# A two-layer hybrid diffusion step: a mark behind the normalisation, modulations shared by halves, and a residual added by DMA

## The chip, the cores and the metric

One core of a Trainium2 chip runs the program. The metric is the device time of one execution in microseconds (us), lower is better; the median of several timed executions is compared.

## The reference

Two layers act on 128 context tokens and 128 latent tokens that share all weights; the model width is 2048 and the feed-forward width 8192, in float32. Cut to what the change touches:

```
mods = silu(cond) @ w_mod[l] + b_mod[l]          # six vectors of 2048 for each kind of token
shift1, scale1, gate1, shift2, scale2, gate2 = mods
h = rms_norm(x, norm1_g) * (1 + scale1) + shift1
mix = concat(gla(h @ w_in), attention(h @ w_in), deltanet(h @ w_in)) @ w_out
x = x + gate1 * mix
h = rms_norm(x, norm2_g) * (1 + scale2) + shift2
x = x + gate2 * (square(relu(h @ w_ff1)) @ w_ff2)
```

`cond` is one vector for the context tokens and one for the latent tokens, so that a modulation is a product of a 2048 x 2048 block of `w_mod` with two vectors. Modulations are numbered m = 0 to 5 in the order above (0 shift1, 1 scale1, 2 gate1, 3 shift2, 4 scale2, 5 gate2); (l, m) is modulation m of layer l. The outputs are x of both kinds of token and the caches and states of the context.

## The kernel before

**Layout and units.** x stays in SBUF, transposed: 16 chunks of 128 model rows by 256 columns, of which the first 128 are context tokens and the last 128 latent ones. A matrix product is made in units of 128 output rows, a unit of the feed-forward in two halves of the contraction. For each half a 512 KB tile `raw` (128x1024) is loaded on SP's queue (`load_half`, six buffers). ACT rounds it to `hi`, DVE forms `lo` = `raw` − `hi` (`split_half`, three buffers each), and PE runs 16 matmuls with `hi` (on the rounded activations and on their remainders) and 8 with `lo`, into the PSUM tile `g` (`gemm_d`). The evacuation of w_out and ff2 (`res_evac`) is DVE's: x += g * gate, one instruction for each kind of token. That of ff1 (`ff_evac`) is three ACT instructions and a DVE subtraction.

**Stages of a layer.** Input projection and the three mixers, then w_out (16 units), a lead stage, and the feed-forward: ff1 in four blocks of 16 units, ff2 in four, in the order ff1(0), ff1(1), ff2(0), ff1(2), ff2(1), ff1(3), ff2(2), ff2(3). In the lead stage (`norm_lead`) PE runs the first six units of ff1 on x as it is before the normalisation (PSUM tile `gl`), and DVE and ACT make the normalised input beside that: `get_rstd` with a Newton iteration of small DVE instructions (`nv`, `n2t`, `n2y`), then `normed`, 16 chunks in each of which DVE makes `ht`, ACT `hu` and the rounded `act`, and DVE the remainder, `act` = `hu` − `act`. The rest of ff1(0) needs those chunks.

**Modulations.** They are filler work, made well before they are needed, on one of two engines. `mod_pe` runs 16 groups on PE, each with two 512 KB loads `raw` from `w_mod` on SP's queue and four matmuls 32x512 (eight rows in the trace); it ends with a small addition of the bias `bm` on DVE. `mod_dv` runs on DVE: for each of two halves of the contraction and each of 16 output chunks it loads a 512 KB tile `mraw` on SP's queue (three buffers) and runs two multiply-and-reduce instructions against the broadcast vectors `sb` (1 MB, one buffer, loaded on POOL's queue at the start of each half). They show as `CUSTOM_DVE_ANT_0 junk` in the trace and as `ISA junk` in the order, 64 for a modulation; the first half starts from `bm` and leaves sums in `part`, the second starts from `part` and writes `modc`. The list `ONDV` says which modulations go to DVE: (0,5), (1,1), (1,0), (1,5).

**What sets the order.** `start_mod` puts a modulation's generator into a queue, `modq` for PE and `modv` for DVE. After every half-unit `tick()` takes one step of each, at the rates in `rate`: for PE R3 = 0.15 in the feed-forward, for DVE V3 = 0.6 in ff1(0) and ff1(1) and V5 = 0.55 behind them; in layer 1 the rate for DVE is 0. All seven modulations of layer 0's feed-forward start behind the first two normalised units of ff1(0): (0,5), then those of layer 1 in the order `FF0M`. `mod_flush` finishes one that is needed. The code's order is only a priority: a scheduler that runs at build time puts each engine's instructions into their final order and may move an instruction whose inputs are there ahead of others. Each engine and queue then runs its own list in order.

Of the kernel before, what the change touches and what calls it, by code (L numbers as in the profile page):

```python
# [17 lines left out]
P = 128  # L18
# [9 lines left out]
V3, V5 = 0.6, 0.55  # L28
FF0M = (1, 0, 5, 2, 4, 3)
MX1M = (4, 3)  # L30
LATE = 3
ONDV = ((0, 5), (1, 1), (1, 0), (1, 5))
# [9 lines left out]
def tile_hybrid_step(ctx: ExitStack, tc: tile.TileContext, A: dict, O: dict):  # L42
# [357 lines left out]
    def mod_dv(l, m, modc, bm):  # L400
        mac = X["mac"]
        part = mdp.tile([P, 16, 2], F32, tag="part", name="part")
        i = ONDV.index((l, m))
        order = [(half, n) for half in range(2) for n in range(16)]
# [7 lines left out]
        for u, (half, n) in enumerate(order):  # L412
# [6 lines left out]
            for c in range(2):  # L419
                junk = mac.tile([P, 1024], BF16, tag="junk", name="junk")  # L420
                ve.tensor_tensor_reduce(
                    out=junk, in0=raw, in1=sb[:, c], scale=1.0,
                    scalar=part[:, n, c : c + 1] if half else bm[:, m, n : n + 1], op0=ALU.mult, op1=ALU.add,
                    accum_out=modc[:, m, n, c : c + 1] if half else part[:, n, c : c + 1],
                )
            yield

    def mod_pe(l, m, modc, bm):
        ps = pmod.tile([P, 512], F32, tag="mod", name="mod")
        tk = newtok()  # L430
        for k in range(16):
            raws = [load_half(A["w_mod"][l, m, k, half]) for half in range(2)]
            for gg in (2, 3, 0, 1):
# [4 lines left out]
                    start=(k == 0),  # L438
# [8 lines left out]
        for r in range(4):  # L447
# [4 lines left out]
            bc(bm[:, m].rearrange("p (g r) -> p r g", r=4), 2),  # L452
# [41 lines left out]
    def normed(rstd, dst, scl, shf):  # L494
        for k in range(16):
# [7 lines left out]
            ve.tensor_tensor(dst[:, k, 256:512], u, dst[:, k, 0:256].bitcast(F32), ALU.subtract)  # L503
# [12 lines left out]
    def start_mod(l, m):  # L516
        modc, s12, bm, ng = mods[l]

        def chain():
            yield from (mod_dv if (l, m) in ONDV else mod_pe)(l, m, modc, bm)  # L520
# [9 lines left out]
        (modv if (l, m) in ONDV else modq).append(g)  # L530
# [112 lines left out]
    for l in range(L):  # L643
# [790 lines left out]
        rate[:] = [R3, 0 if last else V3]  # L1434
# [4 lines left out]
        def ff1(q):  # L1439
            hid = hids[q % 2]  # L1440
            us = [(tsrc(w1, q * 16 + j), ff_evac(hid, j)) for j in range(LEAD if q == 0 else 0, 16)]
            if q == 0:
                d = DL
                gemm_seq(us[:d], lambda k: nact[:, k, 0:512])
                us = us[d:]
                if (l, 5) not in gens:
                    start_mod(l, 5)
                if not last:
                    for m in FF0M:
                        start_mod(l + 1, m)  # L1450
            gemm_seq(us, lambda k: nact[:, k, 0:512])
            return hid

        def ff2(q, hid):
            st = q == 3 and not last
            sc1 = mods[l + 1][1][:, 0] if st else None
            gemm_seq([(tsrc(w2[q], n), res_evac(n, 5, act if st else None, sc1)) for n in range(16)], lambda k: hid[:, k, 0:512], l in WIDE)
# [195 lines left out]
```

## Time and profile before

| | us |
|---|---|
| median of 3 timed runs | 2579.03 |
| lowest and highest | 2578.31, 2583.78 |
| the profiled run | 2589.99 |
| its span (first to last instruction) | 2588.2 |
| its PE, DVE, ACT busy | 2503.7, 1822.5, 1225.7 |

The mean granted TensorE clock of the profiled run is 0.986 of full speed. PE is TensorE's matmuls, PEld its weight loads (they overlap PE), DVE VectorE, ACT ScalarE, POOL GpSimd, SP SyncE. Nearly all instructions are recorded at a few helper lines (L56 for DVE and ACT, L86 for matmuls), so the names of output and inputs tell them apart. Layer 0's w_out stage runs from 506.37 to 606.17 us, its lead to 688.36, its feed-forward to 1410.44; layer 1's w_out stage runs from 1778.71 to 1858.03 and its lead to 1908.97.

### The profile page before, as it was taken

What the parts mean: (1) busy time and instruction counts of PE and PEld (TensorE: products, weight loads), DVE (VectorE), ACT (ScalarE), POOL (GpSimd) and SP (SyncE); (2) the same over time, 40 slices, a digit from 0 to 9 for tenths busy, and PEclk for the clock granted to TensorE, in tenths of its full rate; (3) what the DMA queues carried; (4) which work ended last, traced back from release to release, by engine and by line L of the source; (5) the groups of instructions that cost most, each with busy time, mean ns of one, the idle gap of its engine ahead of it and who ended that gap; (6) DMA issues with size and microseconds to landing.
All of it is one profiled execution on the core that took longest, in us unless ns stands there. A gap on an engine that the chain in (4) does not pass through costs nothing.

```text
span 2588.2 us, 47588 instructions
## 1 busy us (share of the span) xinstructions
PE 2503.7 (97%) x18860; PEld 2250.6 (87%) x18860; DVE 1822.5 (70%) x3510; ACT 1225.7 (47%) x1977; POOL 31.2 (1%) x59
## 2 busy tenths in 40 slices
PE   6999999988799999999999999999999999999999
PEld 4777677778799999999999888898999989999888
DVE  3456767698998889988456767697764565564665
ACT  3356244434655345344344763455575435445433
POOL 1000000000000000000000000000000000000000
PEclk9999999998899999999999999999999999999999
DMA  9875767797799999998777765445556666666664
GB/s 362 313 253 180 274 213 279 274 371 247 241 327 340 326 336 326 333 333 294 235 235 237 245 232 172 141 134 166 176 182 185 185 190 188 185 192 187 185 199 141
DMA packets 171935, 622.00 MB, mean 240 GB/s; under 512 B 20496, under 2 KB 21072, under 8 KB 170688
## 3 DMA queue, kind: packets, MB, share of 16 engines
q1 hardware_dynamic: 165600, 600.12, 68.4%
q0 software_dynamic: 3712, 15.59, 1.7%
q8 instruction: 148, 2.42, 0.4%
q10 hardware_dynamic: 2400, 3.24, 0.4%
q14 instruction: 75, 0.61, 0.1%
HBM read 612.57 MB, written 6.31 MB: 239 GB/s over the span
## 4 chain that ended last, share of the span: by engine, by line
PE 89%; DMA 4%; DVE 3%; ACT 2%; issue 1%; SPq 0%; ACTq 0%; DVEq 0%
PE g L86 67%; PE gt L86 6%; PE mod L86 4%; PE gl L86 4%; DMA raw<-w_mod 2%; DMA raw<-w_tok 1%; DVE lo L56 1%; ACT hi L56 1%; PE ga L86 1%; DVE junk L56 1%; PE eb L86 1%; DMA raw<-w_in 1%; PE fb L86 0%; PE fbm L86 0%; PE ob L86 0%
## 5 line engine op out<-in xcount | busy, mean ns | idle before, releaser
L56 ACT ACTIVATE hi<-raw 128x1024 fp32r<-128x1024 f32 (+1 forms) x742 | 784.5, 1058 | 1104.2 <-PE g L86 791.3
L56 DVE TENSOR_TENSOR lo<-raw,hi 128x1024 fp32r<-128x1024 f32 (+1 forms) x742 | 905.1, 1220 | 431.9 <-ACT hi L56 416.4
L86 PE MATMUL g<-act,hi 128*128 128x256 f32 (+1 forms) x7488 | 1054.1, 291 | 23.9 <-ACT ffr L56 7.4
L86 PEld LDWEIGHTS g<-act,hi 128*128 128x128 f32 x7488 | 955.6, 189 | 100.5 <-ACT hi L56 27.4
L86 PE MATMUL g<-act,lo 128*128 128x256 f32 x4000 | 562.8, 282 | 3.2 <-DVE lo L56 3.2
L86 PEld LDWEIGHTS g<-act,lo 128*128 128x128 f32 x4000 | 516.8, 190 | 14.5 <-DVE lo L56 4.9
L56 DVE SCALAR_TENSOR_TENSOR x<-g,modc,x 128x128 f32<-128x128 f32 x448 | 142.3, 348 | 185.8 <-PE g L86 180.5
L86 PE MATMUL g<-hid,hi 128*128 128x256 f32 (+1 forms) x1536 | 261.3, 319 | 0.0
L86 PEld LDWEIGHTS g<-hid,hi 128*128 128x128 f32 x1536 | 217.1, 188 | 23.1 <-ACT hi L56 5.0
L86 PE MATMUL mod<-raw,sc 128*32 128x512 f32 (+1 forms) x1280 | 152.1, 537 | 28.9 <-DMA raw<-w_mod 25.3
L56 DVE CUSTOM_DVE_ANT_0 junk<-mraw,sb,bm 128x1024 bf16<-128x1024 f32 x128 | 164.0, 1282 | 5.3 <-DMA sb<-scd 2.5
L56 DVE CUSTOM_DVE_ANT_0 junk<-mraw,sb,part 128x1024 bf16<-128x1024 f32 x128 | 164.1, 1282 | 2.1 <-DMA sb<-scd 1.7
L86 PE MATMUL gt<-hi,act 128*128 128x512 f32 x512 | 144.5, 414 | 3.7 <-ACT hi L56 3.7
L86 PE MATMUL g<-hid,lo 128*128 128x256 f32 x1024 | 141.8, 281 | 0.0
L86 PEld LDWEIGHTS g<-hid,lo 128*128 128x128 f32 x1024 | 134.6, 188 | 5.4
L86 PEld LDWEIGHTS gt<-hi,act 128*128 128x128 f32 x512 | 94.6, 192 | 41.1 <-issue 13.7
L86 PEld LDWEIGHTS mod<-raw,sc 128*32 128x32 f32 x1280 | 30.1, 110 | 67.0 <-DMA raw<-w_mod 21.6
L86 PE MATMUL gl<-hid,hi 128*128 128x258 f32 x384 | 74.8, 297 | 4.0 <-ACT hi L56 3.1
L86 PE MATMUL gt<-lo,act 128*128 128x512 f32 x256 | 75.7, 405 | 0.0
L86 PEld LDWEIGHTS gl<-hid,hi 128*128 128x128 f32 x384 | 62.9, 200 | 5.1 <-ACT hi L56 3.7
L86 PE MATMUL gl<-hid,lo 128*128 128x258 f32 x192 | 56.6, 296 | 3.6 <-DVE lo L56 3.6
L86 PEld LDWEIGHTS gt<-lo,act 128*128 128x128 f32 x256 | 48.3, 192 | 10.8 <-issue 0.4
(352 smaller groups left out, 1882.7 us busy)
## 6 DMA issues: line engine op xcount, KB each, us to landing
raw<-w_ff SPq DMA_DIRECT2D x512, 512.0 KB, 4.4
raw<-w_mod SPq DMA_DIRECT2D x256, 512.0 KB, 5.9
mraw<-w_modT SPq DMA_DIRECT2D x128, 512.0 KB, 6.0
raw<-w_in SPq DMA_DIRECT2D x86, 512.0 KB, 4.4
raw<-w_tok SPq DMA_DIRECT2D x64, 512.0 KB, 4.5
raw<-w_out SPq DMA_DIRECT2D x64, 512.0 KB, 4.4
sb<-scd POOLq DMA_DIRECT2D x8, 1024.0 KB, 8.7
raw<-w_in SPq DMA_DIRECT2D x16, 448.0 KB, 6.2
```

The lines of the kernel that those rows point to most:

```text
L56: return f(out, *a, **kw)
L86: i = nc.tensor.matmul(out, lhsT=lhsT, rhs=rhs, start=start, stop=stop, **kw)
```

## The change

Three things change, and two rates with them.

1. A mark. The last subtraction of `normed` and the first multiply-and-reduce instruction of every `mod_dv` get the issue-order token "normed": the scheduler keeps instructions with one token in the order of the code, so a modulation on DVE can't be put ahead of that subtraction.
2. Halves. `mod_dv`, `mod_pe` and `start_mod` take the halves of the contraction they are to make. Of (1,2) DVE makes the first half in layer 0's feed-forward, and PE the second (groups 8 to 15, with `part` added in place of `bm`). Of (1,5), which DVE made whole in layer 0's feed-forward, the second half moves to layer 1's ff1(0), at the new rate V4 = 0.4. V3 becomes 0.65.
3. Adds. In layer 0, ff2 blocks 0 to 2 evacuate with `add_evac`: two ACT copies scaled by the gate write `xd` (128x256, two buffers), and a DMA on POOL's queue adds `xd` to x. The two DVE instructions on x of each of these 48 units are gone.

```diff
--- before.py
+++ after.py
@@ -25,11 +25,11 @@
 TB = 4
 NRAW = 6
 GATES = (4, 5, 6, 7, 0, 1, 2, 3)
-V3, V5 = 0.6, 0.55
-FF0M = (1, 0, 5, 2, 4, 3)
+V3, V5, V4 = 0.65, 0.55, 0.4
+FF0M = ((1, (0, 1)), (0, (0, 1)), (2, (0,)), (5, (0,)), (4, (0, 1)), (3, (0, 1)), (2, (1,)))
 MX1M = (4, 3)
 LATE = 3
-ONDV = ((0, 5), (1, 1), (1, 0), (1, 5))
+ONDV = ((0, 5), (1, 1), (1, 0), (1, 5), (1, 2))
 DL = 2
 WIDE = (1,)
 K0, K1 = 0.4, 0.7
@@ -397,11 +397,15 @@
             if tick():
                 yield
 
-    def mod_dv(l, m, modc, bm):
+    parts = {}
+
+    def mod_dv(l, m, modc, bm, halves):
         mac = X["mac"]
-        part = mdp.tile([P, 16, 2], F32, tag="part", name="part")
+        if 0 in halves:
+            parts[l, m] = mdp.tile([P, 16, 2], F32, tag="part", name="part")
+        part = parts[l, m]
         i = ONDV.index((l, m))
-        order = [(half, n) for half in range(2) for n in range(16)]
+        order = [(half, n) for half in halves for n in range(16)]
 
         def fetch(u):
             raw = mac.tile([P, 1024], F32, tag="mraw", name="mraw", bufs=3)
@@ -418,24 +422,27 @@
             nxt = fetch(u + 1) if u + 1 < len(order) else None
             for c in range(2):
                 junk = mac.tile([P, 1024], BF16, tag="junk", name="junk")
-                ve.tensor_tensor_reduce(
+                i_ = ve.tensor_tensor_reduce(
                     out=junk, in0=raw, in1=sb[:, c], scale=1.0,
                     scalar=part[:, n, c : c + 1] if half else bm[:, m, n : n + 1], op0=ALU.mult, op1=ALU.add,
                     accum_out=modc[:, m, n, c : c + 1] if half else part[:, n, c : c + 1],
                 )
+                if u == 0 and c == 0:
+                    tc.stamp_issue_order_token(i_.ins, "normed")
             yield
 
-    def mod_pe(l, m, modc, bm):
+    def mod_pe(l, m, modc, bm, halves):
         ps = pmod.tile([P, 512], F32, tag="mod", name="mod")
         tk = newtok()
-        for k in range(16):
+        k0 = 8 * halves[0]
+        for k in range(k0, 16):
             raws = [load_half(A["w_mod"][l, m, k, half]) for half in range(2)]
             for gg in (2, 3, 0, 1):
                 mm(
                     ps[32 * gg : 32 * gg + 32, :],
                     sc[:, 2 * k : 2 * k + 32],
                     raws[gg // 2][:, (gg % 2) * 512 : (gg % 2) * 512 + 512],
-                    start=(k == 0),
+                    start=(k == k0),
                     stop=(k == 15),
                     tile_position=(0, 32 * gg),
                     tok=tk,
@@ -449,7 +456,7 @@
         ve.tensor_tensor(
             modc[:, m].rearrange("p (g r) c -> p r g c", r=4),
             pt[:, 0:32].rearrange("p (r g c) -> p r g c", r=4, c=2),
-            bc(bm[:, m].rearrange("p (g r) -> p r g", r=4), 2),
+            parts[l, m].rearrange("p (g r) c -> p r g c", r=4) if k0 else bc(bm[:, m].rearrange("p (g r) -> p r g", r=4), 2),
             ALU.add,
         )
         yield
@@ -500,7 +507,9 @@
                 ve.scalar_tensor_tensor(t[:, s], X["x"][:, k, s], scl[:, k, g : g + 1], rstd[:, s], ALU.mult, ALU.mult)
                 se.activation(u[:, s], t[:, s], AF.Identity, bias=shf[:, k, g : g + 1])
             se.activation(dst[:, k, 0:256], u, AF.Copy)
-            ve.tensor_tensor(dst[:, k, 256:512], u, dst[:, k, 0:256].bitcast(F32), ALU.subtract)
+            i = ve.tensor_tensor(dst[:, k, 256:512], u, dst[:, k, 0:256].bitcast(F32), ALU.subtract)
+            if k == 15:
+                tc.stamp_issue_order_token(i.ins, "normed")
             yield
 
     def norm_lead(srcs, xsp, dst, scl, shf, ldp, sink=None):
@@ -513,11 +522,12 @@
         se.activation(act[:, k, 0:256], src, AF.Copy)
         ve.tensor_tensor(act[:, k, 256:512], src, act[:, k, 0:256].bitcast(F32), ALU.subtract)
 
-    def start_mod(l, m):
+    def start_mod(l, m, halves=(0, 1)):
         modc, s12, bm, ng = mods[l]
+        dv = (l, m) in ONDV and (m != 2 or 0 in halves)
 
         def chain():
-            yield from (mod_dv if (l, m) in ONDV else mod_pe)(l, m, modc, bm)
+            yield from (mod_dv if dv else mod_pe)(l, m, modc, bm, halves)
             if m in (1, 4):
                 j = 0 if m == 1 else 1
                 ve.scalar_tensor_tensor(
@@ -527,7 +537,7 @@
 
         g = chain()
         gens[l, m] = g
-        (modv if (l, m) in ONDV else modq).append(g)
+        (modv if dv else modq).append(g)
         return g
 
     def tsrc(w, n):
@@ -1431,7 +1441,7 @@
 
         norm_lead([tsrc(w1, j) for j in range(LEAD)], hidb, nact, s12[:, 1], modc[:, 3], X["np"],
                   lambda j, t: ff_evac(act, j)(t))
-        rate[:] = [R3, 0 if last else V3]
+        rate[:] = [R3, V4 if last else V3]
         if not last:
             mod_tiles(l + 1)
             layer_consts(l + 1)
@@ -1443,18 +1453,27 @@
                 d = DL
                 gemm_seq(us[:d], lambda k: nact[:, k, 0:512])
                 us = us[d:]
-                if (l, 5) not in gens:
-                    start_mod(l, 5)
+                start_mod(l, 5, (1,) if last else (0, 1))
                 if not last:
-                    for m in FF0M:
-                        start_mod(l + 1, m)
+                    for m, halves in FF0M:
+                        start_mod(l + 1, m, halves)
             gemm_seq(us, lambda k: nact[:, k, 0:512])
             return hid
+
+        def add_evac(n):
+            def f(ps):
+                t = X["np"].tile([P, 256], F32, tag="xd", name="xd", bufs=2)
+                for g in range(2):
+                    s = slice(g * P, g * P + P)
+                    se.activation(t[:, s], ps[:, s], AF.Copy, scale=modc[:, 5, n, g : g + 1])
+                nc.gpsimd.dma_start(x[:, n, :], t, accum_op=ALU.add)
+
+            return f
 
         def ff2(q, hid):
             st = q == 3 and not last
             sc1 = mods[l + 1][1][:, 0] if st else None
-            gemm_seq([(tsrc(w2[q], n), res_evac(n, 5, act if st else None, sc1)) for n in range(16)], lambda k: hid[:, k, 0:512], l in WIDE)
+            gemm_seq([(tsrc(w2[q], n), add_evac(n) if q < 3 and not last else res_evac(n, 5, act if st else None, sc1)) for n in range(16)], lambda k: hid[:, k, 0:512], l in WIDE)
 
         h0 = ff1(0)
         h1 = ff1(1)
```

The order shows where instructions now stand. DVE in layer 0's lead, at the Newton iteration (ISA junk and the small ISA behind it are the modulation); before:

```order
L56 TENSOR_SCALAR nv<-st 128x2
L56 TENSOR_TENSOR lo<-raw,hi 128x1024
L56 ISA junk,modc<-mraw,sb,part 128x1024
L56 ISA modc 128x1
L56 TENSOR_SCALAR n2t<-nv 128x2
L56 ISA junk,modc<-mraw,sb,part 128x1024
L56 ISA modc 128x1
L56 TENSOR_SCALAR n2y<-n2t 128x2
```

and after:

```order
L56 TENSOR_SCALAR nv<-st 128x2
L56 TENSOR_SCALAR n2t<-nv 128x2
L56 TENSOR_SCALAR n2y<-n2t 128x2
L56 SCALAR_TENSOR_TENSOR n2t<-nv,n2y 128x2
L56 TENSOR_TENSOR n2t<-n2t,n2y 128x2
L56 SCALAR_TENSOR_TENSOR n2y<-n2t,n2y 128x2
L56 SCALAR_TENSOR_TENSOR n2t<-nv,n2y 128x2
L56 TENSOR_TENSOR lo<-raw,hi 128x1024
```

The modulation instructions that stood between the Newton steps have moved behind the last subtraction of `normed`; from there to the end of the lead DVE's rows are those of layer 1's lead.

SP's queue around the first load from `w_mod` in layer 0's feed-forward; before:

```order
L408 DMA mraw<-w_modT 128x1024
L212 DMA raw<-w_mod 128x1024
L408 DMA mraw<-w_modT 128x1024
L212 DMA raw<-w_mod 128x1024
L212 DMA raw<-w_ff 128x1024 x2
L408 DMA mraw<-w_modT 128x1024 x2
```

and after:

```order
L212 DMA raw<-w_out 128x1024 x16
L212 DMA raw<-w_ff 128x1024 x21
L212 DMA raw<-w_mod 128x1024
L412 DMA mraw<-w_modT 128x1024
L212 DMA raw<-w_mod 128x1024
L212 DMA raw<-w_ff 128x1024 x4
L412 DMA mraw<-w_modT 128x1024 x2
```

The `mraw` loads that stood among the loads of w_out and of the lead are gone from there, and one now stands between the two `w_mod` loads of a group.

POOL's queue in layer 0's feed-forward (`sb` is the broadcast tile; the rows behind it are of the next stage); before:

```order
L167 DMA lsmall<-lsmall 128x4
L416 DMA sb<-scd 128x2048 x8
L635 DMA csin<-c_rope 128x256
L636 DMA gmask<-c_gmask 128x896
L1008 DMA s0d<-s_dn 128x1024
```

and after:

```order
L420 DMA sb<-scd 128x2048 x2
L1469 DMA x<-xd 128x256
L420 DMA sb<-scd 128x2048
L1469 DMA x<-xd 128x256 x14
L420 DMA sb<-scd 128x2048
L1469 DMA x<-xd 128x256
L420 DMA sb<-scd 128x2048
L1469 DMA x<-xd 128x256 x12
L420 DMA sb<-scd 128x2048
L1469 DMA x<-xd 128x256 x4
```

The 48 adds stand among the loads of `sb` on one queue.

## Rows read from the trace of the kernel before

**Rows 1.** Page, part 1: busy time, share of the span, instructions by engine.

```profile
PE 2503.7 (97%) x18860; PEld 2250.6 (87%) x18860; DVE 1822.5 (70%) x3510; ACT 1225.7 (47%) x1977; POOL 31.2 (1%) x59
```

**Rows 2.** Windows: from:to us, engines' busy us (instructions), PE clock, DMA share, GB/s.

```profile
506.37:606.17 99.80, 92.78 (x744) 83.83 (x745) 90.88 (x165) 43.10 (x75) 0.54 (x1) 0.98 0.95 355
606.17:688.36 82.19, 61.78 (x401) 56.94 (x399) 77.38 (x155) 43.77 (x105) 0.00 (x0) 0.81 0.67 223
688.36:1410.44 722.08, 722.08 (x6040) 689.97 (x6041) 587.29 (x861) 328.83 (x463) 3.19 (x6) 1.00 0.86 301
1410.44:1560.00 149.56, 148.28 (x1106) 124.75 (x1105) 108.70 (x304) 98.29 (x198) 1.08 (x2) 0.99 0.71 246
1778.71:1858.03 79.32, 79.32 (x672) 79.32 (x673) 53.88 (x100) 43.97 (x73) 0.00 (x0) 1.00 0.63 198
1858.03:1908.97 50.94, 47.28 (x393) 46.82 (x391) 42.13 (x94) 41.86 (x105) 0.00 (x0) 1.00 0.53 172
```

**Rows 3.** Groups of DVE, 506.37 to 688.36: xcount | busy, mean ns | idle.

```profile
L56 DVE CUSTOM_DVE_ANT_0 junk<-mraw,sb,bm 128x1024 bf16<-128x1024 f32 x32 | 41.1, 1284 | 0.3
...
L56 DVE CUSTOM_DVE_ANT_0 junk<-mraw,sb,part 128x1024 bf16<-128x1024 f32 x31 | 39.9, 1289 | 0.0
```

**Rows 4.** Timeline of DVE in both leads: start us, us, instruction, output<-inputs.

```profile
615.54 0.17 DVE L56 TENSOR_SCALAR n2t<-nv 128x2 int32<-128x2 int32 x1
615.67 1.28 DVE L56 CUSTOM_DVE_ANT_0 junk<-mraw,sb,part 128x1024 bf16<-128x1024 f32 x1
616.88 0.17 DVE L56 TENSOR_SCALAR n2y<-n2t 128x2 int32<-128x2 int32 x1
...
1900.06 0.42 DVE L56 TENSOR_TENSOR act<-hu,act 128x256 fp32r<-128x256 f32 x1
```

**Rows 5.** Timeline of PE, ends of both leads; brackets: idle time before, its releaser.

```profile
676.18 1.93 PE L86 MATMUL mod<-raw,sc 128*32 128x512 f32 x8 [2.56 <-DMA raw<-w_mod]
...
688.36 3.48 PE L86 MATMUL g<-act,hi 128*128 128x256 f32 x16 [4.76 <-ACT ffr L56]
...
1908.97 2.15 PE L86 MATMUL g<-act,hi 128*128 128x256 f32 x16 [2.63 <-ACT ffr L56]
```

**Rows 6.** Groups of PE in layer 0's w_out stage, 506.37 to 606.17.

```profile
L86 PE MATMUL g<-act,hi 128*128 128x256 f32 x448 | 59.1, 285 | 6.0 <-ACT hi L56 3.8 <-DVE x L56 2.1
...
L86 PE MATMUL mod<-raw,sc 128*32 128x512 f32 x64 | 8.5, 605 | 0.0
```

**Rows 7.** Groups of PE at the start of layer 1, 1410.44 to 1570.

```profile
L86 PE MATMUL mod<-raw,sc 128*32 128x512 f32 x112 | 17.9, 637 | 0.0
```

**Rows 8.** Groups of DVE and ACT in layer 0's feed-forward, 688.36 to 1410.44.

```profile
L56 DVE TENSOR_TENSOR lo<-raw,hi 128x1024 fp32r<-128x1024 f32 x239 | 292.2, 1222 | 65.1 <-ACT hi L56 61.4 <-PE g L86 1.8
L56 DVE CUSTOM_DVE_ANT_0 junk<-mraw,sb,part 128x1024 bf16<-128x1024 f32 x98 | 125.5, 1280 | 2.1 <-DMA sb<-scd 1.7
L56 DVE CUSTOM_DVE_ANT_0 junk<-mraw,sb,bm 128x1024 bf16<-128x1024 f32 x96 | 123.0, 1281 | 5.1 <-DMA sb<-scd 2.5 <-DMA raw<-w_ff 2.3
L56 DVE SCALAR_TENSOR_TENSOR x<-g,modc,x 128x128 f32<-128x128 f32 x126 | 38.4, 347 | 59.9 <-PE g L86 59.8
...
L56 ACT ACTIVATE act<-x,s 128x128 fp32r<-128x128 f32 x30 | 10.4, 395 | 3.5 <-DVE x L56 3.5
```

**Rows 9.** DMA issues: output<-input queue xcount, KB each, median us to landing.

```profile
raw<-w_ff SPq DMA_DIRECT2D x512, 512.0 KB, 4.4
raw<-w_mod SPq DMA_DIRECT2D x256, 512.0 KB, 5.9
...
sb<-scd POOLq DMA_DIRECT2D x8, 1024.0 KB, 8.7
...
o_ck<-akv POOLq DMA_DIRECT2D x2, 128.0 KB, 3.9
```

**Rows 10.** Window of 10 us in layer 0's w_out stage.

```profile
560.00:570.00 10.00, 10.00 (x86) 10.00 (x87) 10.00 (x18) 6.34 (x11) 0.00 (x0) 1.00 1.03 409
```

**Rows 11.** Timeline of POOL, one load of the broadcast tile.

```profile
598.83 0.54 POOL L416 DMA_DIRECT2D sb<-scd  x1 [97.83 <-DVE part L56]
```

## The prediction

> **What bounds the kernel now.** I read the page's busy times first, then the windows by stage, then the groups and timelines of the stage that stands out. TensorE (PE) is busy 97% of the span [rows 1], so time leaves only where PE stands still or where PE work is taken away. The windows [rows 2] show where it stands still. In layer 0's feed-forward (688.36 to 1410.44) PE is busy for all 722.08 us, so a faster DVE or ACT is worth nothing there, and a slower one costs only once it holds PE up. The hole is ahead of it. In layer 0's lead stage (606.17 to 688.36: normalisation, with the first six ff1 units on PE) PE is busy 61.78 of 82.19 us and its granted clock is 0.81 on average. The same stage of layer 1 (1858.03 to 1908.97) takes 50.94 us at clock 1.00. DVE makes the difference: 77.38 us busy against 42.13. The w_out stage ahead (506.37 to 606.17) takes 99.80 us, where layer 1's takes 79.32 for the same 28 half-units; DVE is busy 90.88 of it.
>
> What fills DVE there are the modulation instructions: 32 and 31 of them in these two stages, 81 us [rows 3]. In the lead they stand between the small steps of the Newton iteration on which the normalisation depends. The timeline [rows 4] shows one: the step n2t at 615.54, a 1.28 us junk at 615.67, the step n2y only at 616.88. Layer 1 has none of these at this place. So the hole is a matter of order on DVE; the work itself isn't needed until much later.
>
> **The mark (the token "normed").** The order of the changed kernel has no modulation on DVE ahead of the last subtraction of the normalisation; the Newton steps follow each other, and in the lead its rows are those of layer 1. So layer 1's 50.94 us is the nearest row for the lead. On PE the lead has one modulation group more than layer 1's, 8.5/8 = 1.06 us [rows 6]. It can also meet a new wait: on SP, the second w_mod load of that group now stands behind an mraw load, which needs a buffer that the first two junk instructions free. In layer 1's frame the last subtraction ends at 1900.06 + 0.42 = 1900.5 [rows 4]; two junks and three small steps behind it put the free buffer at about 1904; landing adds 5.9 [rows 9], so 1909.9. PE there waits for ACT until 1908.97 anyhow [rows 5], so about 1 us shows. Lead: 50.9 + 1.1 + 1 = 53, a change of 53 − 82.2 = **−29**. Bounds: −31, if it equals layer 1's; −20, if the two junks (2.6) and the landing (5.9) are exposed in full beyond this. Before, such a mod group already waited 2.56 for its load [rows 5].
>
> In the w_out stage 79.3 of pure matmuls and eight mod groups at 8.5 make 87.8, and 99.80 stands there: 12 us are stalls and slower pieces, 6.0 of it idle before the hi matmuls, of which 3.8 is put down to ACT's hi [rows 6], and DMA runs at share 0.95 [rows 2]. Without some twenty mraw loads and 32 junks I take 7 of the 12 back: **−7**, bounds −4 (roughly the named 3.8) and −11 (nearly all).
>
> **The shared modulations.** Half of modulation (1,2) goes from PE to DVE: 8 groups leave PE. The 33 groups that run in layer 0's feed-forward stay (same rate R3), so the 8 are missing where the rest runs, at the start of layer 1: there 112 rows, 14 groups, cost 17.9, 1.28 each [rows 7], and PE is busy 148.28 of 149.56 us [rows 2]. I take the cheaper 1.06 each, **−8.5**; bounds −10 (1.28 each) and −6 (the mixer's waits take a part).
>
> The DVE side: in the feed-forward of layer 0 there were 98 + 96 = 194 junks [rows 8]; now all 256 of it are there, since none is made ahead: 62 × 1.281 = +79 us. The adds take away 96 residual instructions of 38.4/126 = 0.305 each: −29. DVE goes from 587 to 637 of 722 us, 88%. That is an average; by half-unit, PE needs 79.32/28 = 2.83 plus 0.15 × 1.06, 2.99 us. DVE needs at rate 0.65: lo 1.22, 0.65 × 2 junks × 1.281 = 1.67, half a subtraction 0.21, in all 3.10, for the 48 half-units of the first two ff1 blocks. It falls behind 0.11 × 48 = 5 us in all, beside a stock of three lo buffers (9 us of PE). In the rest (0.55, residuals gone) it needs 2.63 to 2.84 of 2.99. I take **+5**: bounds 0 (the stock covers it) and +15 (5 us, and one load of the broadcast tile sb, 8.7 [rows 9], that isn't covered). A gain is excluded, since PE has no idle time there [rows 2].
>
> In layer 1's first ff1 block 32 junks are new, 41 us over some 33 half-units: 1.22 + 0.4 × 2.56 + 0.21 = 2.45 of 2.83 on DVE, so hidden. As they too wait for the mark and then meet a loaded queue, I take **+2**, bounds 0 and +4.
>
> **The adding DMAs.** 48 units of layer 0's ff2 (blocks 0 to 2) get two ACT copies, 0.395 each by the nearest ACT instruction [rows 8], an issue on POOL's queue of 0.54 [rows 11] and a transfer of 128 KB. ACT is at 329 of 722 us [rows 2], so 38 more fit. No trace row shows an adding DMA. The nearest rows on the same queue: 3.9 us for 128 KB, 8.7 for the 1 MB of sb [rows 9]. The buffer xd is written again two units later, 2 × 5.98 = 12 us. With 0.8 (ACT) + 0.54 + landing, up to 10.6 us of landing are hidden; both rows lie below. What is queued behind the adds on POOL are the sb loads, and ahead of some adds stands an sb load that waits for DVE's last junk of a half (the row shows POOL waiting 97.83 us that way [rows 11]); a few units of delay at four or five such places are in the +5 above. I take **0**.
>
> **Sum:** −29 − 7 − 8.5 + 5 + 2 = −37.5, call it −38. The profiled run took 2589.99 us, 11 above the median of 2579.03, so it would go to 2552; the median to **2541**.
>
> **Rivals.**
> *Only half of the hole closes.* With the junks gone ACT is next: 43.77 us busy in the lead [rows 2], and PE then waits for it as in layer 1. For: layer 0 runs its lead behind a stage with mod loads and a full DMA. Against: layer 1 does the same ACT work in 50.94. Half of the 29 left: −38 + 14, 2555.
>
> *DVE bounds the feed-forward.* The upper bound above, +15 in place of +5: 2551. Against: its average is 88%.
>
> *The transfers bound ff2 of layer 0.* Per half-unit one weight load, 0.55 mraw and 0.3 w_mod loads of 524 KB: 970 KB in 2.99 us, 324 GB/s; an add reads xd, reads x and writes x, 3 × 131 KB in 5.98 us, 66 more: 390. The largest rate kept over a whole stage is 355 GB/s [rows 2], though a 10 us stretch ran at 409 with PE at full clock and busy throughout [rows 10]. If only 355 can be kept, 48 units of 5.98 (287 us) stretch by 390/355: +28, which gives 2569. That row is why I give this rival 0.10 and no more. The Trainium skill ("DMA: Bandwidth & Descriptors", section "Where 436 GB/s comes from") lets HBM's side (about 358 GB/s) bind loads from HBM, and only the fabric (435) bind moves inside SBUF. By it the loads' 324 and the total of 390 would both fit, nothing would be lost, and the chance would be nearer 0.05; but the 409 of the trace, nearly all of it loads from HBM, stands above the page's 358, so the measured rows decide.
>
> *The adds pace ff2, slower than before.* xd has two buffers. Once ACT's writing, the issue and the landing exceed 12 us, ACT stands before the copy, the hi copies queued behind it on ACT come late, and PE stops; a unit then takes (landing + 1.34)/2. It must cost 43 us over the 48 units to be slower by 0.2%: 6.88 a unit, a landing of 12.4. If the three legs of 128 KB go one after the other at 3.9 each, stretched by 5.9/4.4 as loads are in the dense stretches [rows 9], landing is 15.7, a unit 8.5, +121: **2662**. For: no row shows such a transfer. Against: eight times the bytes land in 8.7 on that queue.
>
> **How the numbers follow.** About 0.2%, 5 us, is what a measurement of this kernel can tell from no change. Chances: forecast 0.63, half of the hole 0.10, DVE 0.08, transfers 0.10, pace 0.09. The best bounds together give −31 − 11 − 10 = −52, 2527; the worst ones −20 − 4 − 6 + 15 + 4 = −11, 2568. The range 2526 to 2567 holds the first three and part of the fourth, about 0.8. Faster: 0.63 + 0.10 + 0.08 and some of the transfers' case (0.03), 0.84; same 0.05, the middle of that case; slower 0.11: the pace and the tail of the transfers.
>
> **What the changed profile would show.** The mark: layer 0's lead at about 53 us, PE clock near 1.0, the Newton steps back to back, w_out at 90 to 95 us. The shared modulations: 64 mod rows fewer on PE, 32 junks more on DVE, layer 1's start is 8 to 10 us shorter, and PE stays at 100% in layer 0's feed-forward with DVE near 88%. The adds: 96 x residuals fewer on DVE, and landing stays below 10.6 us. I am wrong if PE's hi matmuls in ff2 wait for ACT behind an xd copy (pace), if raw loads there land much later than 6 us (transfers), if lo holds PE in ff1 (DVE), or if the lead still takes 65 us or more.

## The result

The changed kernel takes 2548.27 us (2546.04 to 2549.01) where the kernel before took 2578.67 (2578.04 to 2583.78): 0.9876 of it, 95% interval 0.9859 to 0.9893, 30 us less. The forecast was 2541, the range 2526 to 2567. Run again (after_again, below), the same pair gave 2547.85 and 2577.41.

By stage, from one profiled execution of it (windows; columns as in [rows 2]):

```profile
497.65:590.32 92.67, 91.40 (x745) 83.49 (x746) 53.54 (x101) 43.93 (x75) 0.00 (x0) 0.98 0.82 296
590.32:643.44 53.12, 49.17 (x400) 47.05 (x398) 46.66 (x103) 43.58 (x110) 0.00 (x0) 0.98 0.56 178
643.44:1370.80 727.36, 723.39 (x6045) 689.84 (x6042) 631.22 (x881) 348.19 (x554) 44.27 (x55) 1.00 0.94 332
1370.80:1737.16 366.36, 360.44 (x2483) 315.87 (x2481) 276.79 (x746) 202.30 (x371) 8.82 (x15) 0.99 0.50 161
1816.86:1867.94 51.08, 47.27 (x393) 46.82 (x391) 44.60 (x99) 41.94 (x105) 0.00 (x0) 1.00 0.56 176
1867.94:2547.20 679.26, 674.06 (x4736) 630.25 (x4736) 422.58 (x612) 309.70 (x412) 0.00 (x0) 1.00 0.62 193
```

They are layer 0's w_out, lead and feed-forward, layer 1's start (which [rows 2] shows only in part; it took 368.27 us before), and layer 1's lead and feed-forward. The lead is 53.12 us at clock 0.98 where it was 82.19 at 0.81, and DVE is busy 46.66 us in it in place of 77.38. The granted clock has two levels, 2.4 and 1.2 GHz, shown as 1.00 and 0.50; a mean of 0.81 is a stage that ran part of its time at the lower one. w_out is 92.67 in place of 99.80. The feed-forward of layer 0 became longer, 727.36 for 722.08, and PE, which was never idle there, now is for 4 us.

The Newton steps, of which [rows 4] showed two with 1.28 us between them, now follow each other at 0.2 us (timeline of DVE; start us, us):

```profile
598.93 0.16 DVE L56 TENSOR_TENSOR n2t<-n2t,n2y 128x2 f32<-128x2 f32 x1
599.12 0.16 DVE L56 SCALAR_TENSOR_TENSOR n2y<-n2t,n2y 128x2 f32<-128x2 f32 x1
599.31 0.16 DVE L56 SCALAR_TENSOR_TENSOR n2t<-nv,n2y 128x2 f32<-128x2 f32 x1
599.51 0.16 DVE L56 TENSOR_TENSOR n2t<-n2t,n2y 128x2 f32<-128x2 f32 x1
599.71 0.16 DVE L56 SCALAR_TENSOR_TENSOR n2y<-n2t,n2y 128x2 f32<-128x2 f32 x1
```

The adds and the other loads on POOL's queue (issues; KB each, median us to landing), which answer to [rows 9]:

```profile
sb<-scd POOLq DMA_DIRECT2D x9, 1024.0 KB, 9.5
...
x<-xd POOLq DMA_DIRECT2D x48, 128.0 KB, 6.9
```

An add lands 6.9 us after its issue in the median and 10.6 at most, the median between the two rows that bounded it (3.9 and 8.7); 10.6 was the landing up to which the prediction had two buffers suffice.

### The profile page after: what moved, and what is told of

The parts are those of the page before. It is cut to its first block, busy times and chain, and to the rows that moved or that the text cites. A ratio compares the mean times of both kernels' runs of the same rounds, so it can differ in the third digit from the quotient of the medians.

```text
span 2547.2 us, 47725 instructions
## 1 busy us (share of the span) xinstructions
PE 2482.5 (97%) x18796; PEld 2240.5 (88%) x18796; DVE 1836.3 (72%) x3478; ACT 1246.1 (49%) x2073; POOL 72.3 (3%) x108
## 3 DMA queue, kind: packets, MB, share of 16 engines
q1 hardware_dynamic: 165600, 600.12, 68.4%
q0 software_dynamic: 10768, 22.94, 3.4%
## 4 chain that ended last, share of the span: by engine, by line
PE 52%; ACT 1%; DVE 0%; DMA 0%; issue 0%; DVEq 0%; ACTq 0%
PE g L86 42%; PE gt L86 3%; PE gl L86 3%; PE mod L86 1%; PE ga L86 0%; ACT hi L56 0%; PE eb L86 0%; PE scb L86 0%; PE oatb L86 0%; PE xt L86 0%; PE yb L86 0%; PE ob L86 0%; PE bcb L86 0%; DMA x<-spill 0%; PE obg L86 0%; ACT L56 0%
## 5 line engine op out<-in xcount | busy, mean ns | idle before, releaser
L56 DVE SCALAR_TENSOR_TENSOR x<-g,modc,x 128x128 f32<-128x128 f32 x352 | 113.1, 348 | 149.5 <-PE g L86 144.3
L56 DVE CUSTOM_DVE_ANT_0 junk<-mraw,sb,bm 128x1024 bf16<-128x1024 f32 x160 | 205.0, 1281 | 2.4 <-DMA sb<-scd 0.9
L86 PE MATMUL mod<-raw,sc 128*32 128x512 f32 (+1 forms) x1216 | 144.1, 530 | 26.3 <-DMA raw<-w_mod 24.4
L56 ACT ACTIVATE ffr<-g 128x256 f32<-128x256 f32 x116 | 42.9, 370 | 55.1 <-PE g L86 55.1
L56 ACT ACTIVATE xd<-g,modc 128x128 f32<-128x128 f32 x96 | 29.7, 360 | 68.1 <-PE g L86 68.1
```

The source lines that it names most:

```text
L56: return f(out, *a, **kw)
L86: i = nc.tensor.matmul(out, lhsT=lhsT, rhs=rhs, start=start, stop=stop, **kw)
```

## The experiments

**Where the first profile misled: the kernel before, again**

> The kernel before, unchanged, profiled once more. Its first profile ran 11 us over the median of its timed runs, and against the profile after it is 8.7 us longer up to layer 0's w_out stage, where the two programs are the same. Theory one: those 8.7 us are an accident of that one execution; w_out begins at about 498 us here, the lead still takes 82 us, the w_out stage 100, and the whole is near 2579. Theory two: the lead and w_out were also longer than usual in the first profile; then they take 75 and 95 here, and the change gained less there than the 36 us read from the two profiles.

It was profiled at 2581.29 us, span 2579.5. Up to w_out, w_out, the lead and the feed-forward of layer 0, and layer 1's start:

```profile
0.00:496.56 496.56, 454.23 (x3337) 345.52 (x3337) 307.21 (x840) 212.57 (x382) 19.25 (x38) 0.99 0.76 269
496.56:596.73 100.17, 91.03 (x745) 82.24 (x745) 90.87 (x165) 43.10 (x75) 0.54 (x1) 1.00 0.96 361
596.73:677.77 81.04, 59.43 (x401) 54.83 (x399) 77.36 (x155) 43.71 (x105) 0.00 (x0) 0.87 0.71 229
677.77:1401.06 723.29, 723.29 (x6041) 691.18 (x6041) 587.92 (x861) 328.74 (x463) 3.19 (x6) 1.00 0.86 301
1401.06:1768.12 367.06, 363.16 (x2547) 313.20 (x2545) 275.54 (x746) 202.07 (x371) 8.23 (x14) 1.00 0.55 183
```

Theory one holds. w_out begins at 496.56, not 506.37, and every later stage is within 1.6 us of the first profile. The same stretch took 490.8 to 500.4 us in the other runs below, and in all of them PE, DVE, ACT and POOL have the same instructions in the same order up to there, so what differs between two profiles is no effect of an edit. The longest and the shortest of them, the first profile of the kernel before and after_again:

```profile
0.00:506.37 506.37, 461.95 (x3337) 349.93 (x3337) 306.80 (x840) 212.74 (x382) 19.26 (x38) 0.97 0.75 265
```

```profile
0.00:490.81 490.81, 451.79 (x3336) 344.67 (x3337) 306.56 (x840) 212.38 (x382) 19.19 (x38) 0.99 0.77 272
```

PE waited for loads of `w_mod` about as long in both (22.7 and 20.1 us), but was busy 10 us longer at a lower mean clock, 0.97 for 0.99. So most of the 15 us is the granted clock. From here on I compare stages, and of totals the timed medians.

**The mark alone**

```diff
+            if k == 15:
+                tc.stamp_issue_order_token(i.ins, "normed")
...
+                if u == 0 and c == 0:
+                    tc.stamp_issue_order_token(i_.ins, "normed")
```

> The kernel before with the mark alone (old rates, old lists, residual on DVE). Theory: the mark is nearly the whole gain. Lead 53 and w_out 93 as after, -36; the 62 junks that it sends into layer 0's feed-forward put DVE at 587 + 79 = 666 of 722 us, which costs 5 to 8: 2550 (2546 to 2554). Rival, the adds are what makes the mark pay: without them DVE (1.22 + 0.55 x 2.56 + 0.31 = 2.94 of 2.99 us a half-unit in ff2) holds PE up, +25 in the feed-forward, 2568.

2548.55 us, 0.9878 (0.9863 to 0.9894) of the kernel before: as much as the whole change. w_out took 92.89 and the lead 52.73 us. Layer 0's feed-forward and layer 1's start:

```profile
644.45:1370.00 725.55, 725.55 (x6045) 690.52 (x6041) 654.87 (x978) 325.90 (x458) 3.71 (x7) 1.00 0.91 325
1370.00:1739.21 369.21, 363.15 (x2546) 314.45 (x2545) 275.48 (x746) 202.35 (x371) 8.19 (x14) 1.00 0.56 182
```

The junks sent here from the two stages ahead put DVE at 654.87 us, 90%, and PE isn't idle in any of the 725.55. The rival is out: the mark needs no adds to pay.

**The change without the mark**

```diff
-            if k == 15:
-                tc.stamp_issue_order_token(i.ins, "normed")
...
-                if u == 0 and c == 0:
-                    tc.stamp_issue_order_token(i_.ins, "normed")
```

> The kernel after without the mark. Theory: the mark is the whole gain; without it the lead takes 80 and w_out 99 again, +34, and the feed-forward has 63 junks fewer, -4: 2578 (2572 to 2584). Rival: halves and adds bring a part of their own, 2565 or less.

2594.8 us, 1.0063 (1.0041 to 1.0085) of the kernel before: slower than that, which neither expectation had. Layer 0's lead and layer 1's lead (windows), and a group of DVE in the second:

```profile
596.42:676.36 79.94, 56.68 (x401) 52.01 (x399) 77.19 (x155) 43.94 (x105) 0.00 (x0) 0.88 0.71 230
1841.96:1911.38 69.42, 53.50 (x392) 51.54 (x391) 57.24 (x121) 42.43 (x107) 0.00 (x0) 0.90 0.55 166
```

```profile
L56 DVE CUSTOM_DVE_ANT_0 junk<-mraw,sb,part 128x1024 bf16<-128x1024 f32 x13 | 16.7, 1282 | 0.0
```

Layer 0's lead is long again, as expected. What neither theory had: 13 junks of (1,5), whose second half the change starts in layer 1's ff1(0), were put into layer 1's lead, and that went from 51 to 69.42 us at clock 0.90, 18.3 more, of which the junks are 16.7. The other 19 of that half stood in layer 1's w_out stage, which at 79.70 us was no longer for them: it is the normalisation that they hold up. So putting work of DVE behind a normalisation in the code makes a second hole unless the mark holds it back. The mark closes one hole and prevents another.

**Without the adds**

```diff
-            gemm_seq([(tsrc(w2[q], n), add_evac(n) if q < 3 and not last else res_evac(n, 5, act if st else None, sc1)) for n in range(16)], lambda k: hid[:, k, 0:512], l in WIDE)
+            gemm_seq([(tsrc(w2[q], n), res_evac(n, 5, act if st else None, sc1)) for n in range(16)], lambda k: hid[:, k, 0:512], l in WIDE)
```

> The kernel after, with the residual of layer 0's ff2 on DVE again. Theory: DVE has room for 96 instructions of 0.305 us (631 + 29 = 660 of 727 us), so within 3 us of the kernel after, 2546 to 2552. Rival A, the adds were needed: +12 or more, with PE waiting for lo in ff2. Rival B, the adds cost (DMA share is 1.00 to 1.04 in the ff2 blocks after): -4, and the feed-forward falls back to 722.

2543.14 us, 0.9865 (0.9849 to 0.9881). That is below the kernel after, but the two aren't known to have run on one chip, so it ran once more:

> The kernel after without the adding DMAs, once more, since adds_only says that they cost 0.12% (0.02 to 0.22) and the first run without them was 5 us under the kernel after. Theory: the adds cost about 3 us, so this is 0.9865 of the kernel before (0.985 to 0.9875), and layer 0's feed-forward is 725 and not 727 to 729. Rival: the difference was one of chips and sessions, 0.9875 to 0.9885.

2542.25 us, 0.9853 (0.983 to 0.9875). Rival B of the first expectation, which the second took as its theory, is the likelier both times; but its intervals and those of the changed kernel (0.9859 to 0.9893, and 0.9859 to 0.99 in after_again) overlap, so the 5 us are not settled by the totals. The stage shows a part of the reason. Layer 0's feed-forward in no_adds_again:

```profile
641.71:1366.47 724.76, 724.76 (x6045) 689.72 (x6041) 654.87 (x977) 325.88 (x458) 3.71 (x7) 1.00 0.91 325
```

PE is never idle, with DVE at 654.87; with the adds DVE is at 631.22 and PE waits 4 us. The waits of PE in the changed kernel's feed-forward (us in total, times, longest), and the longest of them on PE's and on DVE's timeline:

```profile
PE g L86 <- DVE lo L56: 2.8, 2, 2.1
PE g L86 <- ACT hi L56: 1.2, 1, 1.2
```

```profile
904.82 1.21 PE L86 MATMUL g<-act,lo 128*128 128x256 f32 x8 [2.13 <-DVE lo L56]
```

```profile
898.01 0.42 DVE L56 TENSOR_TENSOR act<-ffr,act 128x256 fp32r<-128x256 f32 x1 [3.75 <-ACT ffr L56]
898.35 1.28 DVE L56 CUSTOM_DVE_ANT_0 junk<-mraw,sb,part 128x1024 bf16<-128x1024 f32 x1
...
899.68 1.29 DVE L56 CUSTOM_DVE_ANT_0 junk<-mraw,sb,part 128x1024 bf16<-128x1024 f32 x1
...
901.01 1.28 DVE L56 CUSTOM_DVE_ANT_0 junk<-mraw,sb,part 128x1024 bf16<-128x1024 f32 x1
...
902.34 1.28 DVE L56 CUSTOM_DVE_ANT_0 junk<-mraw,sb,part 128x1024 bf16<-128x1024 f32 x1
...
903.55 1.22 DVE L56 TENSOR_TENSOR lo<-raw,hi 128x1024 fp32r<-128x1024 f32 x1
```

Four junks stand in a row ahead of a lo for which PE waits, some 20 us behind the change from ff2(0) to ff1(2). DVE was idle 3.75 us just before them. So it isn't a lack of DVE time: the order came out with the junks in a clump. That the clump comes from the adds is what comparing the traces suggests (without the adds no wait is left); it wasn't tried by itself.

The two profiles of this one kernel also show what the granted clock does to a stage. Layer 1's start in no_adds, two stretches of it, and one row of 16 matmuls in the first stretch:

```profile
1371.23:1737.33 366.10, 358.51 (x2482) 315.47 (x2481) 276.86 (x746) 202.36 (x371) 8.73 (x15) 0.99 0.50 160
1430.40:1437.20 6.80, 6.80 (x31) 5.12 (x32) 2.09 (x7) 3.83 (x9) 0.00 (x0) 0.50 0.88 287
1720.50:1723.90 3.40, 3.40 (x21) 3.07 (x23) 2.82 (x15) 1.79 (x3) 0.00 (x0) 0.50 0.02 5
```

```profile
1433.86 3.64 PE L86 MATMUL g<-act,hi 128*128 128x256 f32 x16
```

The same stage and the same row in no_adds_again:

```profile
1366.47:1728.07 361.60, 353.80 (x2482) 311.77 (x2481) 276.67 (x746) 201.73 (x371) 8.74 (x15) 1.00 0.51 162
```

```profile
1427.73 2.16 PE L86 MATMUL g<-act,hi 128*128 128x256 f32 x16
```

In no_adds the clock stood at 0.50 for 10.2 us, and the stage is 4.5 us longer. Just ahead of the first stretch PE ran small matmuls and was idle 0.37 us, ahead of the second it was idle 1.18 us; in no_adds_again it was idle 0.37 and 1.17 us at the same places, and the clock stayed at 1.00. So one profile's stage can be 4 to 5 us longer by the clock alone, and when the clock falls isn't shown. Below, the time at clock 0.50 stands beside a stage where it matters.

**The adds alone, in the kernel before**

```diff
+        def add_evac(n):
...
-            gemm_seq([(tsrc(w2[q], n), res_evac(n, 5, act if st else None, sc1)) for n in range(16)], lambda k: hid[:, k, 0:512], l in WIDE)
+            gemm_seq([(tsrc(w2[q], n), add_evac(n) if q < 3 and not last else res_evac(n, 5, act if st else None, sc1)) for n in range(16)], lambda k: hid[:, k, 0:512], l in WIDE)
```

> The kernel before with the adding DMAs alone. Theory: they are worth nothing or cost a little: the lead stays at 81, DVE loses 29 us in layer 0's feed-forward where it is no bound, and that stage goes from 723 to 723 to 727: within 4 us of the kernel before. Rival A: unloading DVE helps, -5 or more. Rival B: the transfers are near their limit (350 GB/s at share 1.0 in ff2 after), +8 or more.

2583.11 us, 1.0012 (1.0002 to 1.0022): the theory, at its dearer end. Layer 0's feed-forward was 722.8 us in the profile, which doesn't show where the 3 us went. Taking 29 us off an engine that nobody waits for is worth nothing.

**One buffer for the adds**

```diff
-                t = X["np"].tile([P, 256], F32, tag="xd", name="xd", bufs=2)
+                t = X["np"].tile([P, 256], F32, tag="xd", name="xd", bufs=1)
```

> The kernel after, with one buffer xd in place of two. Theory (the pacing of the fourth rival): a unit of ff2 then takes ACT's 0.72, the issue's 0.84 and the landing's 6.9, 8.5 in place of 5.9 us, 48 times, +120: 2670, with PE waiting for hi in ff2 behind ACT's xd. Rival: ACT's hi runs far enough ahead, or the copy is put off, so that PE hardly waits: within 10, 2558.

2590.65 us in one execution, span 2588.8. Layer 0's feed-forward, and what ACT's copies and PE waited for in it:

```profile
643.97:1416.19 772.22, 739.60 (x6044) 700.93 (x6041) 634.04 (x882) 353.51 (x554) 44.34 (x55) 0.98 0.91 313
```

```profile
ACT xd L56 <- DMA x<-xd: 73.4, 31, 5.8
...
PE g L86 <- ACT xd L56: 23.6, 14, 3.1
```

The pacing that was my slower rival exists: ACT stands before xd until the add has landed (31 times for 48 adds), and PE waits behind ACT. Its price was overestimated, +45 us and not +120. An add landed 6.3 us after its issue here, and that time begins with the issue, so the 0.84 was counted twice: 0.63 for the copies and 6.3, with the gap between them, is some 7.1 a unit in place of 5.9, 48 times 58. With two buffers there are 12 us for these 7.5 (0.63 + 6.9), so the mechanism is far from its point.

**Without the shared halves**

```diff
-FF0M = ((1, (0, 1)), (0, (0, 1)), (2, (0,)), (5, (0,)), (4, (0, 1)), (3, (0, 1)), (2, (1,)))
+FF0M = ((1, (0, 1)), (0, (0, 1)), (5, (0, 1)), (2, (0, 1)), (4, (0, 1)), (3, (0, 1)))
-ONDV = ((0, 5), (1, 1), (1, 0), (1, 5), (1, 2))
+ONDV = ((0, 5), (1, 1), (1, 0), (1, 5))
...
-                start_mod(l, 5, (1,) if last else (0, 1))
+                if not last:
+                    start_mod(l, 5)
```

> The kernel after, with modulations (1,2) whole on PE and (1,5) whole on DVE in layer 0, as before. Theory: the start of layer 1 is bound by the chain of the mixers, and groups taken from PE there come back as waits: the eight groups cost 2 us when put back, 2550 (2547 to 2553), and the start is 368 us as in the kernel before. Rival, the prediction's: eight groups of 1.06 are on the path, +8.5, 2557.

2551.94 us, 0.9899 (0.9881 to 0.9916), some 4 us over the changed kernel, with intervals that overlap. Layer 1's start was 367.85 us, the theory's, but layer 0's feed-forward took 731.17, which neither had. In that stage PE is idle 3.9 us, as in the changed kernel; 11.2 us of it ran at clock 0.50, where the changed kernel's two profiles have 1.5 and 7.4, so its extra length needs no effect of the halves. Layer 1's start at full clock, here and in one_xd, which is the changed kernel but for a buffer in layer 0's ff2:

```profile
1377.10:1744.95 367.85, 363.59 (x2546) 313.08 (x2545) 275.12 (x746) 202.14 (x371) 8.28 (x14) 1.00 0.56 183
```

```profile
1416.19:1777.67 361.48, 355.39 (x2483) 311.83 (x2481) 276.49 (x746) 201.30 (x371) 8.82 (x15) 1.00 0.51 163
```

By these the halves are worth 6.4 us there, nearer to the rival's 8.5 than to the theory's 2. The theory's 2 came from the first profile of the changed kernel, whose start has 10.2 us at clock 0.50:

```profile
1430.00:1436.80 6.80, 6.80 (x31) 5.14 (x32) 2.06 (x7) 3.82 (x9) 0.00 (x0) 0.50 0.92 333
1720.10:1723.50 3.40, 3.40 (x20) 3.07 (x21) 2.82 (x15) 1.75 (x3) 0.00 (x0) 0.50 0.02 5
```

**The price of a modulation group on PE**

> The kernel after, unchanged, on the chip of the three runs below, so that they are compared with it there: 2548 (2545 to 2552), lead 53, feed-forward 727, start of layer 1 366.

2547.85 us, 0.9879 (0.9859 to 0.99): w_out 92.18, lead 53.43, feed-forward 729.18, start of layer 1 363.26.

```diff
-R1, R2, R3 = 0.9, 0.45, 0.15
+R1, R2, R3 = 0.9, 0.45, 0.08
```

> The kernel after, with R3 = 0.08 in place of 0.15: 17 of the modulation groups on PE leave layer 0's feed-forward for the start of layer 1. Theory: in the feed-forward PE is the bound and a group costs its 1.06 us, 17 of them 18; at layer 1's start the chain of the mixers is the bound and a group costs about 0.2 (8 groups fewer made it 1.9 shorter), 17 of them 4. Feed-forward 709, start 370, the whole 2534 (2530 to 2540). Rival, as the prediction had it: a group costs 1.06 wherever it is, so nothing changes, 2548.

2546.86 us, 0.988 (0.986 to 0.9899): no change, as the rival said, but not for its reason alone. Feed-forward and start:

```profile
643.63:1348.40 704.77, 704.77 (x5912) 687.26 (x5913) 632.09 (x884) 351.38 (x558) 44.36 (x55) 1.00 0.93 320
1348.40:1739.54 391.14, 377.72 (x2619) 316.66 (x2617) 277.05 (x747) 203.06 (x372) 8.81 (x15) 0.99 0.58 193
```

The start has 22 groups in place of 6. Against the two profiles of the changed kernel the feed-forward lost 22.6 to 24.4 us for 15 groups, the lead 2 for one, and the start gained 24.8 to 27.9 for 16: some 1.6 each in both places, of which PE's waits of 4 us, gone from the feed-forward, are a part. In the start PE is idle 13.4 us in place of 6, and busy 17 to 20 us longer, 1.1 to 1.3 for each of the 16 groups: about their own price, and new waits beside it. So I tried a move that leaves the start with 13 groups, nearly as many as it had before the change, without the adds:

```diff
-R1, R2, R3 = 0.9, 0.45, 0.15
+R1, R2, R3 = 0.9, 0.45, 0.115
...
-            gemm_seq([(tsrc(w2[q], n), add_evac(n) if q < 3 and not last else res_evac(n, 5, act if st else None, sc1)) for n in range(16)], lambda k: hid[:, k, 0:512], l in WIDE)
+            gemm_seq([(tsrc(w2[q], n), res_evac(n, 5, act if st else None, sc1)) for n in range(16)], lambda k: hid[:, k, 0:512], l in WIDE)
```

> The kernel after without the adds and with R3 = 0.115: six modulation groups move from layer 0's feed-forward to the start of layer 1, which then has 13, as many as before the change. Theory: up to 14 groups the start's price is low (8 groups between 366 and 368 us), above that it is high (22 groups: 391), and in the feed-forward a group costs 1.06 or more: -6 to -9 there, +3 at the start, so 2539 (2535 to 2543; 0.9845 to 0.986 of the kernel before). Rival: the price at the start is the same 1.06 as in the feed-forward, 2543 to 2546.

2547.94 us, 0.9879 (0.9864 to 0.9893): my theory fails. The feed-forward fell to 715.03, 10 below no_adds, and the start rose to 377.76, 12 to 16 above it:

```profile
640.39:1355.42 715.03, 715.03 (x5984) 686.83 (x5985) 649.61 (x976) 327.15 (x462) 3.70 (x7) 1.00 0.90 319
1355.42:1733.18 377.76, 365.05 (x2548) 316.50 (x2545) 277.71 (x751) 202.53 (x371) 8.74 (x15) 0.99 0.54 176
```

The low price that the theory started from was mostly the clock's doing (above). Against no_adds, whose start has the same 10.2 us at clock 0.50, PE is busy 6.5 us longer here for seven groups more (six from the feed-forward, one from the lead), 0.9 each, and idle 5.1 us longer. With 14 groups the start took 367 to 370 us in the kernel before, mark_only, no_share and adds_only; PE was idle 4 to 6 us of it, and 12.7 here. So beside the groups' own time there are new waits. That they come from where the groups now stand among the mixers' steps is likely, since the scheduler places them anew with each rate; which placement costs them stays open.

The last run, as its edit against mid115:

```diff
-V3, V5, V4 = 0.65, 0.55, 0.4
+V3, V5, V4 = 0.6, 0.5, 0.5
-FF0M = ((1, (0, 1)), (0, (0, 1)), (2, (0,)), (5, (0,)), (4, (0, 1)), (3, (0, 1)), (2, (1,)))
+FF0M = ((1, (0, 1)), (0, (0, 1)), (2, (0,)), (4, (0, 1)), (3, (0, 1)), (2, (1,)))
-                start_mod(l, 5, (1,) if last else (0, 1))
+                start_mod(l, 5, (0, 1))
```

> As mid115, and modulation (1,5) whole in layer 1's ff1 (V4 = 0.5; V3 = 0.6, V5 = 0.5 in layer 0): 32 junks fewer in layer 0's feed-forward, 32 more in layer 1's. Theory: the 3 to 5 us that the feed-forward of layer 0 lost to DVE's and the queues' load come back, and layer 1's ff1 has room (1.22 + 0.5 x 2.56 + 0.21 = 2.71 of 2.83 us a half-unit): 2 to 4 below mid115. Rival: that loss doesn't hang on the junks; equal to mid115, or 3 above it where ff1 of layer 1 waits for lo.

2548.09 us, 0.9877 (0.9863 to 0.9891), equal to mid115: the rival. Layer 0's feed-forward went from 715.03 to 711.36 us and the start gave 3 back (380.73, with 13.6 us at clock 0.50), but with the 32 junks one modulation group also left the feed-forward for the start, so the two stages don't price the junks alone. Layer 1's feed-forward took 682.52, 1.7 more than in mid115. No arrangement of these rates beat the change without its adds, which has the lowest medians of the kernels run: 2542 to 2543 us, against 2548 for the changed kernel.

## Why the prediction was right, and where it wasn't

By stage, two profiles each (before and before_again; after and after_again), against the terms of the sum:

| stage | before | after | measured, mean | predicted |
|---|---|---|---|---|
| layer 0, w_out | 99.80, 100.17 | 92.67, 92.18 | −7.6 | −7 |
| layer 0, lead | 82.19, 81.04 | 53.12, 53.43 | −28.3 | −29 |
| layer 0, feed-forward | 722.08, 723.29 | 727.36, 729.18 | +5.6 | +5 |
| layer 1, start | 368.27, 367.06 | 366.36, 363.26 | −2.9 | −8.5 |
| layer 1, the rest | 809.49, 811.38 | 810.04, 811.14 | +0.2 | +2 |

The sum is −33.0 by these profiles, −30.4 by the timed medians, and was −37.5 in the prediction. The 2 us for the 32 new junks in layer 1 didn't come.

**The mark.** Right in mechanism and size. Layer 1's lead as the row to go by gave 53 us, and the lead took 53.12 and 53.43; the mod group in it waited for its load as in [rows 5] (2.92 us in the changed kernel). mark_only shows that this part is the whole gain. The sum for the group in the lead (1.1 of work and 1 of waiting) holds too: in r3_low and mid115, which have none there, the lead took 51.09, 2.0 to 2.3 less. Of the 28 us some 17 are PE's idle time, 20.4 and 21.6 us before and 4.0 and 4.2 after; most of the rest is the clock, whose mean was 0.81 and 0.87 while PE stood waiting in the lead. In w_out the 7.6 came as forecast, but the loads and the junks left it together, and no run tells which of them had cost it.

**The halves.** The term of layer 1's start was mis-sized: −8.5, of which −2.9 came by the two pairs of profiles. Over all profiles it is −5.0: with 14 groups and R3 = 0.15 the start took 367.1 to 369.9 us in five, with 6 it took 361.5 to 366.4 in six. Between profiles without a stretch at clock 0.50 in it (before_again, adds_only and no_share; no_adds_again and one_xd) it is −6.7, or 0.8 for each group, inside the bounds of −10 and −6. The step that failed was to take the groups' own time, 1.06 each, as all that changes. PE's idle time rose, from 3.8 and 3.9 us in the two profiles before to 5.9 and 6.0 after: groups partly fill time that the mixers' chain leaves, and [rows 2] with PE busy 148.28 of 149.56 shows only the first part of the stage. And the clock, which the term left out, stood at 0.50 for 10.2 and 3.4 us after, for 3.4 and 0 before; by the 4.5 us for 10.2 in no_adds an estimate is 2 us in the mean. That taking groups away makes the clock fall isn't shown. In the feed-forward, where PE is busy 100% in [rows 2], a group was worth more than its own 1.06 (10 us for six groups in mid115, where PE had no waits to lose); why stays open.

**The feed-forward.** The +5 came out, for another reason than given, so that its size fits is partly luck. I expected DVE to fall behind in the first two ff1 blocks. PE had no wait there; its waits stood at the start of ff1(2), behind a clump of junks, and once in ff1(3), for ACT's hi. By the prediction's own sign (lo holds PE in ff1) that is the DVE rival, at 2.8 us. Without the adds the stage took 724.8 to 725.3 us and PE never waited: +2 is the junks' (and the queues') share, and the other 2 to 4 are the adds' (after_again's 729.18, the upper end, has 7.4 us at clock 0.50). DVE's load was foreseen at 637 us and measured at 631.

**The adds.** I took 0. They cost about 3 us alone (1.0012 of the kernel before, 1.0002 to 1.0022) and some 5 in the changed kernel by the medians of two runs without them, of which the stage shows 2 to 4. That they can bring nothing followed from PE's 722.08 of 722.08; that they cost was left out, since I looked at the transfer and at POOL's queue and not at what the scheduler makes of a freed DVE. That this is where the cost comes from is likely by the clump and not shown by a run.

**The rivals.** The hole closed in full. DVE didn't bound the feed-forward at 90%. The transfers didn't either. Two stretches of 50 us in ff2(0) of the changed kernel:

```profile
793.44:843.44 50.00, 50.00 (x420) 47.08 (x419) 41.73 (x53) 22.04 (x35) 7.72 (x10) 1.00 1.02 351
...
806.00:856.00 50.00, 50.00 (x423) 48.05 (x422) 44.93 (x59) 22.23 (x35) 7.58 (x9) 1.00 1.05 375
```

PE is busy throughout at share 1.02 and 1.05, at 351 and 375 GB/s, and nothing waits. The forecast's 390 can't be set beside these: it counts an add as three times 131 KB, and the trace counts it once (POOL's queue moved 22.94 MB for 15.59 before, 7.35 more for 48 adds and one sb). By the trace's count the forecast is 324 + 22 = 346, and the prediction's ratio 390/355 set two ways of counting against each other. In time of the DMA engines an add isn't cheap: by the pages' shares some 1.6% of the engines' span for 6.3 MB of adds, where SP's loads took 68.4% for 600 MB, so about twice as much for a byte. The pacing is real, and a landing of 6.9, or 10.6 at most, doesn't reach it; its formula adds the issue to a landing that is measured from the issue, as in one_xd. The range held for its main term: the errors, 5.6 in the halves and 3 to 5 in the adds, lie on the same side, and part of the second was in the +5.

## What to carry to other kernels

Where a scheduler fills an engine's idle time with work that isn't urgent, look at short dependent steps on that engine: fillers of 1.28 us between steps of 0.16 us cost 28 us in one stage, and the same stage elsewhere in the program without the filler gives the price of the cure. A stage's busy share doesn't say what work taken out of it gives back: eight groups of 1.06 us gave 6.7 where PE was busy 99% in a chain of small matmuls, and six gave 10 where it was busy 100%. Read the granted clock beside a stage before a difference of a few us is put down to an edit: two profiles of one kernel differed by 4.5 us in one stage. And don't unload an engine that nobody waits for: it gains nothing, and the new order may cost.

## What the runs showed of the hardware

The first 500 us of this program differ between profiles of equal code by 15 us (490.8 to 506.4), at nearly equal waits for loads and a mean granted clock of 0.99 and 0.97; a single profile's total can't settle a question of 10 us in this kernel. In a stretch at clock 0.50 (1.2 GHz) a row of 16 matmuls took 3.64 us that took 2.16 at 1.00; with 10.2 us at 0.50 a stage of 362 us was 4.5 us longer than without, in the same kernel. An adding DMA of 128 KB inside SBUF took 6.9 us from issue to landing in the median, in between the plain 128 KB and 1 MB transfers on its queue, and its issue 0.84 us of POOL where that of a plain load of sb takes 0.54 to 0.56.
